# SSD layer: the output projection's first token tile in four steps, y a step sooner, sample state decay inside VectorE's addition

## The chip, the cores and the metric

The kernel runs on one core of a Trainium2 chip. The time is the device time of one launch in microseconds, the median over runs; a run with a profile adds a trace of one execution. The five engines are TensorE (PE in the rows, its weight loads PEld), VectorE (DVE), ScalarE (ACT), GpSimd (POOL) and SyncE (SP), which here issues the DMAs.

## The reference

One inference step of a two-layer decoder: a Mamba-2 SSD layer, then a latent attention (MLA) layer, with a prompt of 1024 tokens and 8 samples of 8 tokens each that go on from a stored state. All is float32. The change lies in the SSD layer (h is 1024 wide, the inner width 2048, 32 heads of 64, 8 groups of 4 heads, state 128, conv of 4 taps):

```python
def ssd_mixer(h, conv_buf, ssm_state, w_in, conv_w, conv_b, dt_bias, a_log, d_skip, norm_w, w_out):
    proj = jnp.einsum('btd,de->bte', h, w_in)                     # z | x B C | dt
    xbc, new_buf = causal_conv(xbc, conv_buf, conv_w, conv_b)     # 4 taps along time
    xbc = jax.nn.silu(xbc)
    ...
    y, new_state = ssd_scan(xs, dt, a_head, bm, cm, ssm_state)    # by chunks of 128 tokens
    # per chunk: s = dec * s + st
    y = (y + d_skip[:, None] * xs) * jax.nn.silu(z)
    y = y * rsqrt(mean(y * y, per group) + eps) * norm_w
    return einsum('bte,ed->btd', y, w_out), new_buf, new_state    # added to h
```

The layer that follows takes h again, normalised, through its own input weights.

## The kernel before, in words

A float32 product is done as three matmuls of rounded halves: each operand x is split into xh (a cast, on ScalarE or by helper line L130) and xl = x - xh (VectorE or GpSimd, helper line L131), and xh*wh, xh*wl and xl*wh are added in a PSUM bank. The order of the instructions on each engine is the order in which the code is written; nothing moves them later. PSUM has eight banks: two tr, two pj, and one each of cb, y, pv and st.

*The groups.* `ssd_groups` runs the groups g = 1 to 7 in 21 steps t each. In a step stand side by side the input projection and conv of group g (`Flow`: matmuls into pj; conv taps on VectorE, L617; Silu on ScalarE, L626 to L631; z, the gate) and the scan of group g-1 (`Scan`). The scan has eight chunks of 128 prompt tokens and a ninth of the 64 sample tokens, two steps for a chunk. At an even step TensorE does `front(i+1)` (transposes into trp, L703 to L706; cb, L708), at an odd one `back(i)` (the chunk's state st, L89; its output py, L759 and L89). Between them ScalarE does the exponentials M (L734, L740) and casts Ch, xddh and Sh, VectorE adds and multiplies (S, y, xD), GpSimd the low halves. The result y of a chunk is stored to DRAM (y_d), and its squares are summed per token (yssq).

In steps 12 to 20 the scan handles the states of the eight samples, four tiles n of 128 x 4 x 128: `turn_state` (PE, into a tr bank named s0p, L856), `split_state` (halves sh and sl; and GpSimd multiplies the state by its decay, L864), `use_state` (products into pv, L877), `next_state` (a product into the st bank, named sn, L882) and `add_state` (VectorE, s = s + sn, L886). sn and the chunks' st share the one st bank. `third(q)` splits, on VectorE (L826, L829), the sample inputs that `next_state` takes.

*The output projection.* After group 7's projection a last loop of 43 steps runs the scan of group 7 (its first 22 steps) with the product y x w_out. This is cut in two over the inner width: oa takes w_out's chunks 0 to 7 (groups 0 to 3; tag a), ob the chunks 8 to 15 (tag b), each over nine token tiles (eight of 128, one of 64). oa starts from x, and ob from what oa has stored in h_d. For a tile i with first step T(i), each step a half hf of 512 columns:

- `load_y` three steps ahead (SP, yt from y_d), `load_x` one ahead;
- `scale` two ahead (ScalarE, four times 128x256, L1016), and in the same step `turn` (eight PE transposes into both tr banks, ytp, L1026);
- `split` one ahead (yh on ScalarE, yl on VectorE);
- `proj`: 24 matmuls of 128x512 into a pj bank (poa or pob, L101), then the eviction that adds the bank to xr (VectorE), and `store` to h_d two steps after the first.

`WOut` brings w_out: a chunk of 128 x 1024 is loaded into a ring of raws (wraw, L1075, 512 KB each), multiplied by the norm weight and cast to woh (ScalarE, L1080), and VectorE makes wol (`low`, L1086). oa's first step is A0 = 5 and ob's B0 = 23: the eight chunks of oa are split in steps 0 to 3, two a step, and the last six of ob in steps 21 and 22.

*What follows.* The MLA layer first turns h (L235, from xt) and multiplies it by its input weights (wraw from in_mla_w_in, L273). The first three tiles of h are loaded during ob's last tiles.

Of the kernel before, what the change touches and what calls it, by code (L numbers as in the profile page):

```python
# [17 lines left out]
D = 1024  # L18
# [506 lines left out]
class Flow:  # L525
# [75 lines left out]
    def ew(self, t):  # L601
# [10 lines left out]
        if t > 11:  # L612
            bi, j = 3, t - 14
# [58 lines left out]
class Scan:  # L672
# [185 lines left out]
    def split_state(self, n):  # L858
        k, q, pr = self.k, *divmod(n, 2)
        self.sh, self.sl = (self.tile([128, 512], "s" + x, f"s{x}{self.g}{n}", 1, F32R) for x in "hl")  # L860
        split(k, self.sh, self.sl, self.s0p)
        h0 = 4 * self.g + 2 * pr
        s0 = self.s0[n]
        k.nc.gpsimd.tensor_tensor(s0, s0, k.decs[:, h0 // 2, 4 * q : 4 * q + 4].unsqueeze(2).to_broadcast([128, 4, 128]),  # L864
                                  op=ALU.mult)
# [19 lines left out]
    def add_state(self, n):  # L885
        self.k.nc.vector.tensor_tensor(self.s0[n], self.s0[n], self.sn.rearrange("p (b n) -> p b n", b=4), op=ALU.add)  # L886

    def ew(self, t, mid=None):
# [14 lines left out]
        if t == 14:  # L903
            self.third(1)
# [25 lines left out]
        if t == 11:  # L930
            self.third(0)
# [62 lines left out]
class OutProj:  # L994
    def __init__(self, k, ypools, ws, psum, k0, load, tag):
        self.k, self.yp, self.ws, self.psum, self.k0, self.load, self.tag = k, ypools, ws, psum, k0, load, tag
# [5 lines left out]
    def load_y(self, i):  # L1002
        k, (t0, m) = self.k, TILES[i]
        y = self.y[i] = self.yp[i].tile([128, self.ng, 256], F32, tag="yt", name=f"yt{self.tag}{i}", bufs=1)
        k.nc.sync.dma_start(y[:m].rearrange("p g c -> p (g c)"),
                            k.y_d[t0 : t0 + m, self.k0 * 128 : (self.k0 + self.nk) * 128])

    def load_x(self, i):
        yp = self.yp[i]
        xr = self.xr[i] = yp.tile([128, D], F32, tag="xr", name=f"xr{self.tag}{i}", bufs=YHB[yp.name])  # L1010
# [18 lines left out]
    def split(self, i):  # L1029
        yp, m = self.yp[i], TILES[i][1]  # L1030
        nb = YHB[yp.name]
        yh, yl = self.yhl[i] = [yp.tile([128, self.nk, 128], F32R, tag="y" + x, name=f"y{x}{self.tag}{i}", bufs=nb)
# [5 lines left out]

    def proj(self, i, hf):
        nc, m = self.k.nc, TILES[i][1]  # L1040
        c = slice(hf * 512, hf * 512 + 512)
        p = self.psum.tile([128, 512], F32, tag="pj", name=f"po{self.tag}{i}{hf}", bufs=PB["pj"])
        (yh, yl), ws, xr = self.yhl[i], self.ws, self.xr[i]
        drain(mm_tok(nc, p, m, 512, [(yh[:, kk, :m], yl[:, kk], yh[:, kk], ws[kk][0][:, c], ws[kk][1][:, c])
                                     for kk in range(self.nk)]))

# [10 lines left out]
    def ew(self, t):  # L1057
        for d, f in ((2, self.store), (-3, self.load_y), (-2, self.scale), (-1, self.load_x), (-1, self.split)):
            i, odd = divmod(t - d, 2)
            if not odd and 0 <= i < 9:  # L1060
                f(i)

    def pe(self, t):
        i, odd = divmod(t + 2, 2)
        if not odd and 0 <= i < 9:
            self.turn(i)


class WOut:
# [3 lines left out]
    def load(self, kk):  # L1073
        raw = self.raw[kk] = load_raw(self.raws, 1, D, self.bufs)[:, 0]
        self.k.nc.sync.dma_start(raw, self.k.I["ssd_w_out"][0][kk * 128 : kk * 128 + 128])  # L1075

    def split(self, kk, pool):
        nc, raw = self.k.nc, self.raw.pop(kk)
        hi, lo = (pool.tile([128, D], F32R, name=f"wo{x}{kk}") for x in "hl")
        nc.scalar.activation(hi, raw, AF.Copy, scale=self.k.ssdn[:, kk : kk + 1])  # L1080
        self.late.append((raw, hi, lo, kk))
        return hi, lo
# [8 lines left out]
def YORD(yb, ya):  # L1091
    return (yb, ya) * 4 + (yb,)


A0, B0 = 5, 23
# [8 lines left out]
def ssd_groups(k, g0, nxt, pools, sp, psum, st, left, right, als):  # L1104
# [6 lines left out]
    for g in range(1, G):  # L1111
        fl, nxt = nxt, Flow(k, g + 1, pools) if g < G - 1 else None
        nscan = Scan(k, fl, (sp, psum))
        for t in range(21):
# [22 lines left out]
            if t == 18 and not nxt:  # L1137
                als.close()
                wrs = ExitStack()
# [12 lines left out]
    ya = st.enter_context(open_pool(tc, name="ya", bufs=1))  # L1152
    wx = st.enter_context(open_pool(tc, name="wox", bufs=1))
    wsa, wsb = [], []
    oa = OutProj(k, (ya,) * 9, wsa, psum, 0, x_loader(k), "a")
    ob = None
    for t in range(B0 + 20):
        ev = None
        for o, T in ((oa, A0), (ob, B0)):
            u = t - T  # L1160
            if o and 0 <= u < 18:
                ev = o.proj(*divmod(u, 2))
        if t < 22:
            scan.ew(t)
        if t == 0:
            pscan.ew(21)
        if t < 4:
            for kk in (2 * t, 2 * t + 1):
                wsa.append(wo.split(kk, wa))
        if t in (5, 6):  # L1170
            wsb.append(wo.split(t + 3, wx))
        if t < 7:
            wo.low()
            for kk in ((3, 4), (5, 6), (7, 8), (9,), (), (), ())[t]:
# [1158 lines left out]
```

## Time and profile before

| | |
|---|---|
| median of three runs | 2117.57 us (2114.17, 2117.57, 2123.74) |
| profiled execution | 2121.48 us, its span 2119.7, mean granted clock of TensorE 0.955 |
| the groups' loop, g = 1 to 7 | about 150 to 843 us |
| the last loop | 843 to 1140, oa until 1020, ob after |
| MLA | 1140 to the end |

A row of a timeline or of the chain has the start in us, the duration in us, the engine and line, what is written from what, and the size; in square brackets stands how long the engine was idle before it and what ended that. A row of the waits has the engine and line that waited, the line waited for, the total in us, how many times, and the longest. A row of a group of instructions has least, median and largest duration in ns, the first and the last start, and the sizes.

### The profile page before, as it was taken

The numbers are of one execution on the slowest core, as the hardware profiler recorded it, in microseconds if no ns is written. First come the engines' busy times: TensorE is split into PE (matmuls) and PEld (weight loads), VectorE is DVE, ScalarE is ACT, GpSimd is POOL, SyncE is SP. The second block draws the span as 40 slices with busy tenths as digits, with TensorE's granted clock in tenths as the row PEclk, the third lists the DMA queues.
The fourth block names the chain that finished last, engine by engine and source line by source line (L and its number), as shares of the span: only waits on it lengthen the run. The fifth ranks groups of instructions, "written<-read, shape, count | busy, mean of one in ns | idle before, by whom it ended". The sixth has DMA issues, their size and how long they took to land.

```text
span 2119.7 us, 33702 instructions
## 1 busy us (share of the span) xinstructions
PE 1947.4 (92%) x12001; PEld 1776.3 (84%) x12001; DVE 1239.8 (58%) x2556; ACT 1110.2 (52%) x2627; POOL 799.8 (38%) x993
## 2 busy tenths in 40 slices
PE   6989999999999999589798999699999999889998
PEld 5879999999999998477687998698888788768887
DVE  4427574757575666534324314366787878776665
ACT  5346666565656666533325324234676667745553
POOL 0327464746464575332000001102333334655551
PEclk9989999999999999699999999899999999989999
DMA  4113322223323333443455332132111212454441
GB/s 143 40 37 89 90 84 83 89 87 87 88 79 90 90 89 103 145 147 126 145 163 168 122 147 66 52 105 69 47 45 40 63 37 78 131 163 139 143 146 44
DMA packets 186479, 206.56 MB, mean 97 GB/s; under 512 B 23132, under 2 KB 151912, under 8 KB 185928
## 3 DMA queue, kind: packets, MB, share of 16 engines
q1 hardware_dynamic: 181480, 185.40, 29.0%
q0 software_dynamic: 4752, 18.88, 2.8%
q8 instruction: 95, 1.56, 0.3%
q14 instruction: 72, 0.59, 0.1%
q10 hardware_dynamic: 80, 0.13, 0.0%
HBM read 151.05 MB, written 53.28 MB: 96 GB/s over the span
## 4 chain that ended last, share of the span: by engine, by line
PE 63%; DVE 12%; ACT 8%; issue 7%; DMA 5%; POOL 4%; SPq 1%; POOLq 0%; DVEq 0%; ACTq 0%
PE pj L89 22%; PE pq L101 5%; PE poa L101 4%; PE pob L101 4%; PE py L759 2%; PE pj L101 2%; POOL kvl L1981 2%; PE pz L101 1%; PE pk L101 1%; ACT acc L626 1%; PE p L101 1%; PE vp L89 1%; DVE tl L1700 1%; PE kp L89 1%; PE st L89 1%
## 5 line engine op out<-in xcount | busy, mean ns | idle before, releaser
L89 PE MATMUL pj<-xh,wih 128*128 128x384 f32 (+1 forms) x768 | 255.7, 337 | 9.4 <-ACT xh L236 4.8
L89 PE MATMUL pj<-xl,wih 128*128 128x384 f32 (+1 forms) x768 | 254.8, 332 | 0.0
L89 PE MATMUL pj<-xh,wil 128*128 128x384 f32 (+1 forms) x768 | 253.1, 330 | 0.0
L131 DVE TENSOR_TENSOR wil<-wraw,wih 128x512 fp32r<-128x512 f32 x88 | 71.0, 809 | 181.4 <-ACT wih L130 181.4
L1700 POOL TENSOR_TENSOR tl<-P,th 128x384 fp32r<-128x384 f32 (+1 forms) x96 | 90.4, 942 | 181.9 <-ACT P L1698 142.6
L89 PEld LDWEIGHTS pj<-xh,wih 128*128 128x128 f32 x768 | 146.2, 191 | 11.0 <-ACT xh L236 5.8
L617 DVE SCALAR_TENSOR_TENSOR acc<-raw,vec,acc 128x1112 f32<-128x1112 f32 x84 | 148.7, 1770 | 0.2
L89 PEld LDWEIGHTS pj<-xl,wih 128*128 128x128 f32 x768 | 146.7, 191 | 0.6
L89 PEld LDWEIGHTS pj<-xh,wil 128*128 128x128 f32 x768 | 146.2, 190 | 0.0
L101 PE MATMUL pj<-wih,xh 128*128 128x256 f32 x504 | 145.6, 293 | 0.0
L101 PE MATMUL pj<-wil,xh 128*128 128x256 f32 (+1 forms) x504 | 141.1, 286 | 0.0
L1697 ACT ACTIVATE th<-st 128x512 fp32r<-128x512 f32 x192 | 94.1, 490 | 72.8 <-PE st L1693 54.7
L101 PE MATMUL pj<-wih,xl 128*128 128x256 f32 x448 | 128.3, 286 | 0.0
L796 POOL TENSOR_TENSOR y<-y,xD 128x256 f32<-128x256 f32 x64 | 83.7, 1308 | 92.2 <-DVE y L795 86.2
L131 POOL TENSOR_TENSOR xddl<-xdd,xddh 128x256 fp32r<-128x256 f32 x64 | 60.7, 948 | 134.6 <-ACT xddh L130 134.6
L1981 POOL TENSOR_TENSOR kvl<-pgr,kvh 128x1024 fp32r<-128x1024 f32 x32 | 77.9, 2434 | 78.8 <-ACT kvh L1980 78.8
L101 PEld LDWEIGHTS pj<-wih,xh 128*128 128x128 f32 x504 | 98.5, 195 | 0.0
L130 ACT CAST Ch<-acc 128x128 fp32r<-128x128 f32 x56 | 16.9, 302 | 153.2 <-PE py L89 153.2
L734 ACT ACTIVATE M<-M,tok 128x128 f32<-128x128 f32 (+1 forms) x288 | 90.5, 388 | 11.3 <-DMA M<-acs_d 11.3
L101 PEld LDWEIGHTS pj<-wil,xh 128*128 128x128 f32 (+1 forms) x504 | 95.2, 189 | 0.6
L1698 ACT ACTIVATE P<-st 128x512 f32<-128x512 f32 x192 | 93.2, 486 | 0.0
L101 PEld LDWEIGHTS pj<-wih,xl 128*128 128x128 f32 x448 | 87.6, 195 | 0.0
(999 smaller groups left out, 6436.4 us busy)
## 6 DMA issues: line engine op xcount, KB each, us to landing
wraw<-in_ssd_w_in SPq DMA_DIRECT2D x92, 256.0 KB
M<-acs_d SPq DMA_DIRECT2D x64, 256.0 KB
y_d<-xD SPq DMA_DIRECT2D x64, 128.0 KB
s<-in_state_ssm SPq DMA_DIRECT2D x32, 256.0 KB
out_s_ssm<-s SPq DMA_DIRECT2D x32, 256.0 KB
wraw<-in_ssd_w_out SPq DMA_DIRECT2D x16, 512.0 KB
q_d<-qt SPq DMA_DIRECT2D x32, 192.0 KB
qp<-q_d SPq DMA_DIRECT2D x8, 768.0 KB
```

Of the source, the lines that this page charges most:

```text
L89: nc.tensor.matmul(out, a, b, start=(i == 0), stop=(i == n - 1))
L101: nc.tensor.matmul(o, a, b, start=(j == 0), stop=(j == len(ops) - 1))
L131: (eng or nc.vector).tensor_tensor(lo, src, hi.bitcast(F32), op=ALU.subtract)
L617: nc.vector.scalar_tensor_tensor(acc, self.raw[bi][:, j : j + n], k.convw[j][:, blk : blk + 1], acc, op0=ALU.mult, op1=ALU.add)
L626: nc.scalar.activation(acc[:, :, :SEQ], acc[:, :, :SEQ], AF.Silu)
L734: nc.scalar.activation(M[:m, h, :m], M[:m, h, :m], AF.Relu, bias=c.tk[:, 0, 4 * g + h : 4 * g + h + 1], scale=-1.0)
L759: nc.tensor.matmul(py[:m, h * 64 : h * 64 + 64], c.M[:m, h, :m], c.xdt[:m, h * 64 : h * 64 + 64], start=True, stop=True)
L796: nc.gpsimd.tensor_tensor(y[:m], y[:m], c.xD[:m], op=ALU.add)
L1697: nc.scalar.activation(th[:, :n], ps[:, :n], AF.Exp, scale=SCALE)
L1698: nc.scalar.activation(P[:, :n], ps[:, :n], AF.Exp, scale=SCALE)
L1700: eng.tensor_tensor(tl[:, :n], P[:, :n], th[:, :n].bitcast(F32), op=ALU.subtract)
L1981: nc.gpsimd.tensor_tensor(rl, raw, rh.bitcast(F32), op=ALU.subtract)
```

## The change

In the groups: the fourth block's three conv taps move from steps 14, 15, 16 to 15, 16, 17; the Silu of the first pair of blocks goes to step 16 from 17, and one of z's two to step 17 from 19; `third(0)` stands at the start of step 11 and not at its end. The decay of the sample states leaves GpSimd: `add_state` does s = s * dec + sn in four VectorE instructions, one for each sample, with the decay as a scalar per partition.

```diff
-            bi, j = 3, t - 14
+            bi, j = 3, t - 15
...
-        if t in (17, 18):
-            acc, xs = self.xc[t - 17]
+        if t in (16, 18):
+            acc, xs = self.xc[t // 2 - 8]
...
-        if t == 19:
-            for z in self.z[:2]:
-                nc.scalar.activation(z, z, AF.Silu)
+        if t in (17, 19):
+            z = self.z[t // 2 - 8]
+            nc.scalar.activation(z, z, AF.Silu)
...
-        k.nc.gpsimd.tensor_tensor(s0, s0, k.decs[:, h0 // 2, 4 * q : 4 * q + 4].unsqueeze(2).to_broadcast([128, 4, 128]),
-                                  op=ALU.mult)
...
     def add_state(self, n):
-        self.k.nc.vector.tensor_tensor(self.s0[n], self.s0[n], self.sn.rearrange("p (b n) -> p b n", b=4), op=ALU.add)
+        q, pr = divmod(n, 2)
+        c, s0 = (4 * self.g + 2 * pr) // 2, self.s0[n]
+        for b in range(4):
+            self.k.nc.vector.scalar_tensor_tensor(s0[:, b], s0[:, b], self.k.decs[:, c, 4 * q + b : 4 * q + b + 1],
+                                                  self.sn[:, 128 * b : 128 * b + 128], op0=ALU.mult, op1=ALU.add)
...
-        if t == 14:
-            self.third(1)
+        if t in (11, 14):
+            self.third(t == 14)
```

On VectorE, in the scan of group 1 from step 14 to 15, before (y and xD are the chunk's output, acc the conv's sum, s the sample state, sl its low half):

```order
L794 TENSOR_TENSOR y_6_3464<-py_6_3397,tok 128x256
L795 TENSOR_TENSOR y_6_3464<-y_6_3464,py_6_3397 128x256
L617 SCALAR_TENSOR_TENSOR acc_3033<-raw_3043,vec,acc_3033 128x1112
L886 TENSOR_TENSOR s_3153<-s_3153,sn_3480 128x512
L131 TENSOR_TENSOR sl_3510<-s0p_3475,sh_3509 128x512
L721 TENSOR_TENSOR xdt_8_3518<-trp_8_3470,tok 64x256
L727 TENSOR_TENSOR cbm_8_3520<-cb_8_3473,masks 64x64
L803 TENSOR_TENSOR xD_6_3390<-y_6_3464,z_2324 128x256
L617 SCALAR_TENSOR_TENSOR acc_3033<-raw_3043,vec,acc_3033 128x1112
```

and after:

```order
L794 TENSOR_TENSOR y_6_3471<-py_6_3404,tok 128x256
L795 TENSOR_TENSOR y_6_3471<-y_6_3471,py_6_3404 128x256
L885 SCALAR_TENSOR_TENSOR s_3161<-s_3161,decs,sn_3486 128x128 x4
L131 TENSOR_TENSOR sl_3519<-s0p_3481,sh_3518 128x512
L721 TENSOR_TENSOR xdt_8_3526<-trp_8_3476,tok 64x256
L727 TENSOR_TENSOR cbm_8_3528<-cb_8_3479,masks 64x64
L803 TENSOR_TENSOR xD_6_3397<-y_6_3471,z_2328 128x256
L617 SCALAR_TENSOR_TENSOR acc_3041<-raw_3051,vec,acc_3041 128x1112
```

The first tap of acc now stands behind the state's addition and the split of the next state.

In the output projection: each tile's `scale` comes a step ahead of its `turn`, and `load_y` five ahead. A tile 0 takes four steps in place of two: `part(q)` does both halves of two chunks, 12 matmuls, and holds both pj banks; tile i from 1 on starts at T + 2 + 2i. A0 is 1 and B0 is 21. The first tile of a is loaded at step 18 of group 7, scaled at 20, turned right after the last projection of group 7 and split in step 0.

```diff
+        self.start = [T] + [T + 2 + 2 * i for i in range(1, 9)]
...
+    def part(self, q):
+        nc, ws = self.k.nc, self.ws
+        yh, yl = self.yhl[0]
+        if q == 0:
+            self.po = [self.bank(0, hf) for hf in range(2)]
+        for hf, p in enumerate(self.po):
+            c = slice(hf * 512, hf * 512 + 512)
+            for kk in (2 * q, 2 * q + 1):
+                wh, wl = (x[:, c] for x in ws[kk])
+                for j, (a, b) in enumerate(((yh, wh), (yh, wl), (yl, wh))):
+                    nc.tensor.matmul(p, a[:, kk], b, start=(kk + j == 0), stop=(kk == 7 and j == 2))
+        if q == 3:
+            return [self.evict(0, hf, p) for hf, p in enumerate(self.po)]
+        return []
...
-        for d, f in ((2, self.store), (-3, self.load_y), (-2, self.scale), (-1, self.load_x), (-1, self.split)):
+        for d, f in ((-1, self.split), (-3, self.scale), (-1, self.load_x), (-5, self.load_y)):
...
-A0, B0 = 5, 23
+A0, B0 = 1, 21
```

w_out has four raws ahead and not three: chunks 0 to 3 are loaded at step 18 of group 7, 4 to 7 in steps 0 and 1; 8 and 9 at step 8, split at 10 and 11; 10 and 11 loaded there, split at 21; 12 to 15 all loaded at 21 into four raws, split at 22 and 23, into the tiles of a's chunks. y has one ring of two for a and b.

```diff
-                wo = WOut(k, wrs.enter_context(open_pool(tc, name="wor", bufs=1, side="right")), 3)
-                for kk in range(3):
-                    wo.load(kk)
+                wo = WOut(k, wrs.enter_context(open_pool(tc, name="wor", bufs=1, side="right")), 4)
+                wo.load(0, 1, 2, 3)
+            if t == 20 and not nxt:
+                oa.scale(0)
...
+    oa.turn(0)
...
+            w2, wo = wo, WOut(k, st.enter_context(open_pool(tc, name="wor3", bufs=1, side="right")), 4)
+            wo.load(12, 13, 14, 15)
+            ob.ws += w2.split(wa, 10, 11)
+            w2.low()
+        if t in (22, 23):
+            ob.ws += wo.split(wa, 2 * t - 32, 2 * t - 31)
+            wo.low()
...
-        if ev:
-            ev()
+        if t >= B0:
+            evs += ob.work(t)
         if t < 21:
             scan.pe(t)
+        if A0 <= t < A0 + 4:
+            evs += oa.work(t)
+        for ev in evs:
+            ev()
```

On TensorE, at the end of group 7's steps and the start of the last loop, before (sn ends group 6's scan, trp, cb, st and py are the scan of group 7, pj and poa are projections):

```order
L101 MATMUL pj_20_10499<-wil,xh 64x256
L101 MATMUL pj_20_10499<-wih,xh 128x256
L882 MATMUL sn_10546<-bb6True,x36True 128x512
L703 MATMUL trp_1_10585<-ident,acc_9766 128x128
L704 MATMUL trp_1_10585<-ident,acc_9766 128x128
L706 MATMUL trp_1_10585<-ident,acc_9359 128x128
L708 MATMUL cb_1_10589<-acc_9359 128x128
L89 MATMUL st_0_10626<-xddh_0_10564,BTh_0_10528 128x256
L89 MATMUL st_0_10626<-xddl_0_10565,BTh_0_10528 128x256
L89 MATMUL st_0_10626<-xddh_0_10564,BTl_0_10529 128x256
L759 MATMUL py_0_10627<-xdt_0_10531,M_0_10372 128x64 x4
```

and after:

```order
L878 MATMUL sn_10607<-bb6True,x36True 128x512
L1025 MATMUL ytpa_10609<-ident,yta_10485 128x128 x4
L1025 MATMUL ytpa_10614<-ident,yta_10485 128x128 x4
L703 MATMUL trp_1_10666<-ident,acc_9814 128x128
L704 MATMUL trp_1_10666<-ident,acc_9814 128x128
L706 MATMUL trp_1_10666<-ident,acc_9407 128x128
L708 MATMUL cb_1_10670<-acc_9407 128x128
L89 MATMUL st_0_10707<-xddh_0_10632,BTh_0_10585 128x256
L89 MATMUL st_0_10707<-xddl_0_10633,BTh_0_10585 128x256
L89 MATMUL st_0_10707<-xddh_0_10632,BTl_0_10586 128x256
L759 MATMUL py_0_10708<-xdt_0_10588,M_0_10424 128x64 x4
L1050 MATMUL poa_10716<-woh_10652,yha_10644 128x512
```

Tile 0's eight transposes now stand ahead of the scan's second front, and its first products (12 in all, of which the first is shown) right behind the first chunk's py.

On ScalarE, in the scan's fifth chunk before (yta is a tile of y to be scaled, yha its high half):

```order
L130 CAST Ch_5_11104<-acc_9359 128x128
L734 ACTIVATE M_5_11029<-M_5_11029,tok 128x128 x4
L804 ACTIVATE y_3_11042,yssq<-xD_3_10963 128x256
L1016 ACTIVATE yta_11048<-yta_11048,yssq 128x256 x4
L740 ACTIVATE M_5_11029<-M_5_11029 128x512
L130 CAST xddh_5_11180<-xdd_5_11100 128x256
L130 CAST Sh_4_11185<-S_5_11090 128x256
L130 CAST yha_11199<-ytpa_11139 128x512
L130 CAST yha_11199<-ytpa_11144 128x512
```

and after, in the third chunk, where tile 1 of a is split:

```order
L130 CAST Ch_3_10938<-acc_9407 128x128
L734 ACTIVATE M_3_10846<-M_3_10846,tok 128x128 x4
L804 ACTIVATE y_1_10859,yssq<-xD_1_10799 128x256
L740 ACTIVATE M_3_10846<-M_3_10846 128x512
L130 CAST xddh_3_11004<-xdd_3_10934 128x256
L130 CAST Sh_2_11009<-S_3_10924 128x256
L130 CAST yha_11019<-ytpa_10965 128x512
L130 CAST yha_11019<-ytpa_10970 128x512
L1015 ACTIVATE yta_10877<-yta_10877,yssq 128x256 x4
L716 COPY xsT_4_11067<-trp_4_11033 128x256
L719 CAST BTh_4_11069<-trp_4_11033 128x128
```

The four scales stood behind the M of the chunk and ahead of the split of the same tile; now they are those of the next tile and come behind the split.

At the MLA start SP issued the first in_mla_w_in loads right behind the store of ob's tile 7 and ahead of tile 8's; after the change they stand behind both.

More of the change, by code (lines that the diff above doesn't have):

```diff
@@ L1071, in __init__, with load, split @@
         self.k, self.raws, self.bufs, self.raw, self.late = k, raws, bufs, {}, []
[L1073 to L1082, printed above, removed]
+    def load(self, *kks):
+        for kk in kks:
+            raw = self.raw[kk] = load_raw(self.raws, 1, D, self.bufs)[:, 0]
+            self.k.nc.sync.dma_start(raw, self.k.I["ssd_w_out"][0][kk * 128 : kk * 128 + 128])
+    def split(self, pool, *kks):
+        nc = self.k.nc
+        out = []
+        for kk in kks:
+            raw = self.raw.pop(kk)
+            hi, lo = (pool.tile([128, D], F32R, tag=f"wo{x}{kk % 8}", name=f"wo{x}{kk}", bufs=1) for x in "hl")
+            nc.scalar.activation(hi, raw, AF.Copy, scale=self.k.ssdn[:, kk : kk + 1])
+            self.late.append((raw, hi, lo, kk))
+            out.append((hi, lo))
+        return out
     def low(self):
```

129 lines of the change are left out of this document (60 added, 69 removed).

## The prediction

> **What bounds the kernel now.** I read the page first, then four stretches of the span in the windows view, then who TensorE waits for in each of them, and last the chain of waits and the timelines at the places that the change touches.
>
> ```profile
> span 2119.7 us, 33702 instructions
> PE 1947.4 (92%) x12001; PEld 1776.3 (84%) x12001; DVE 1239.8 (58%) x2556; ACT 1110.2 (52%) x2627; POOL 799.8 (38%) x993
> ```
>
> TensorE is busy 92% of the span, so only its idle time and its slow-clock time can be won. The stretches below are the eight groups' loop from 150 us, the start and middle of the output projection's loop, its second half, and the start of the MLA layer (columns: us, PE, PEld, DVE, ACT, POOL, granted clock, DMA share, GB/s).
>
> ```profile
> 150.00:843.00 693.00, 672.92 (x4929) 661.54 (x4927) 451.78 (x780) 426.44 (x1131) 403.20 (x574) 0.99 0.30 87
> 843.00:1045.00 202.00, 155.87 (x771) 126.73 (x770) 89.25 (x162) 84.71 (x206) 55.26 (x78) 0.86 0.44 140
> 1045.00:1140.00 95.00, 95.00 (x447) 77.33 (x446) 22.74 (x37) 22.80 (x49) 0.90 (x2) 1.00 0.48 153
> 1140.00:1180.00 40.00, 32.65 (x179) 28.79 (x178) 24.30 (x43) 25.69 (x49) 3.19 (x3) 0.91 0.64 209
> ```
>
> The groups leave 20.1 us idle, the projection's first 202 us leave 46.1 idle and 28 more to a clock of 0.86 (0.14 x 202), its second half leaves nothing, and the MLA start leaves 7.4. That is the room: about 100 us, of which this change aims at most.
>
> **The groups (taps a step later, no POOL decay, third(0) earlier).** What TensorE waits for between 150 and 843:
>
> ```profile
> PE st L89 <- DVE s L886: 12.7, 7, 1.8
> PE s0p L856 <- DVE b L829: 4.4, 7, 0.7
> PE pv L877 <- DVE sl L131: 2.7, 6, 0.5
> ```
>
> Those 19.8 us are nearly the whole 20.1, seven times each, once per group. One group in the timelines of VectorE, GpSimd and TensorE, with two windows after it:
>
> ```profile
> 309.53 3.99 DVE L617 SCALAR_TENSOR_TENSOR acc<-raw,vec,acc 128x1112 f32<-128x1112 f32 x1
> 313.44 0.67 DVE L886 TENSOR_TENSOR s<-s,sn 128x512 f32<-128x512 f32 x1
> 315.44 1.36 DVE L617 SCALAR_TENSOR_TENSOR acc<-raw,vec,acc 128x1112 f32<-128x1112 f32 x1
> 311.31 1.03 POOL L864 TENSOR_TENSOR s<-s,decs 128x512 f32<-128x512 f32 x1
> 314.26 0.35 PE L89 MATMUL st<-xddh,BTh 128*128 128x256 f32 x1 [1.81 <-DVE s L886]
> 314.00:318.00 4.00, 3.74 (x27) 3.77 (x28) 3.97 (x10) 1.08 (x4) 0.57 (x1) 0.71 0.34 98
> 318.00:322.00 4.00, 4.00 (x31) 3.85 (x31) 1.82 (x3) 0.88 (x2) 2.18 (x2) 0.86 0.22 66
> ```
>
> The conv tap of step 14 stands in VectorE's queue ahead of the addition to the sample state, takes 3.99 us there against 1.36 for the tap two steps on, and the one st bank comes free only after it: TensorE stands 1.81 us. Then the clock is below full for two windows (0.29 x 4 + 0.14 x 4 = 1.7 us lost). With the tap behind the addition the state is added up to 3.99 us sooner, more than the 1.81 that TensorE waits, so this wait goes: 12.7. What is late next is the tap itself: the last one moves to step 17, but the Silu that needs it is that of acc1 in step 18, and the other Silu is moved ahead to share out ScalarE's work. The pv wait shrinks, since sl stands behind the same tap: I take 1 of 2.7. The s0p wait is for a bank that the last product of third(0) frees, which now comes ahead of front1 on VectorE; what front1 issues is then late by the same 0.4 to 0.7 us, so I take 2 of 4.4. The clock is 0.99 over 693 us, 7 us lost in all; seven windows like the two above would be 12, so I take the 7. Sum 22.7, and I say 22.
>
> The new addition costs VectorE four instructions of 128x128 with a scalar operand in place of one of 0.67 us. Before has none of this size; the nearest of this operation is
>
> ```profile
> L237 DVE SCALAR_TENSOR_TENSOR xl<-xtp,vec,xh x24: 550/617/619, 17.5 to 56.6; 128x384 fp32r<-128x384 f32 x16, 128x320 fp32r<-128x320 f32 x8
> ```
>
> 67 ns per 64 columns: about 0.35 us at 128 columns, 1.4 for four, so 0.7 more than now, 32 times. Below, four cost at least what one does (0.67); above, four times 0.55. It lies in a stretch where VectorE works 452 of 693 us, and is less than the tap that leaves its place, so I put it at nothing on the path. The GpSimd multiply (1.03 each) leaves an engine that is idle 40% here: nothing by itself, but fewer stretched taps. Ends for the groups: 27 (all waits and clock), and 10 (the taps, up to 3.99 us long, hold up TensorE at another place for half of what they do now).
>
> **The start of the last loop.** What TensorE waits for between 843 and 1045, three of its rows, then pieces of the chain of waits, then one window in the columns above:
>
> ```profile
> PE ytpa L1026 <- ACT yta L1016: 19.5, 6, 7.9
> PE ytpb L1026 <- ACT ytb L1016: 10.2, 1, 10.2
> PE trp L703 <- DVE yla L131: 2.7, 1, 2.7
> ```
>
> ```profile
> 851.43 1.05 ACT woh L1080
> 855.01 4.25 DMA wraw<-in_ssd_w_out
> 861.74 2.18 ACT woh L1080 x2
> 865.91 6.25 DMA yta<-y_d
> 872.18 1.71 ACT yta L1016 x4
> 878.77 7.20 PE poa L101 x24
> 892.83 7.00 PE poa L101 x24
> 900.38 5.49 PE poa L101 x24
> ```
>
> ```profile
> 860.00:870.00 10.00, 3.32 (x14) 3.06 (x14) 6.80 (x11) 6.97 (x14) 4.64 (x6) 0.50 0.75 220
> ```
>
> Here TensorE has little to do and runs at 0.50, since no product of the projection may begin before all eight halves of w_out are split and tile 0 is loaded, scaled and turned; then it does tile 0's 48 products in two pieces at that clock or near it (7.20 and 7.00 against 5.49). After the change these 48 lie in the four steps of the split, 12 behind each two chunks. The loads of w_out (four raws ahead, not three) take away the 4.25, and tile 0 loaded in group 7 the 6.25. What is left is ScalarE's queue, in order, from where woh began: tile 0's scale and the casts of its split come ahead of it (1.7 and about 1, so 851.4 becomes 854.2), eight woh of 1.09 (8.7), tile 1's scale (1.7), and the scan's own work (6.97 busy in that window less four woh leaves 2.6 for two steps; with its waits for VectorE I put 7 for four): 871.6. Then the fourth step's exponentials, casts and state, from the end of the scale to the first product 4.9 us before (873.9 to 878.8): 876.5. Twelve products at half clock take about 5 (24 took 7.20 and 5.49, part warm and warm, so 2.7 to 3.6 at those clocks and 5.5 at twice the warm time): 881.5. The decay matrices' loads on SP now stand behind four chunks at once; I add 3 for them, near the 4.25 that a chunk cost here, so tile 1 begins near 885 and not 900.4: 15, and I take **14** for a turn more on the way. Ends: 25 (all waiting gone, clock full) and 5 (the chunks' transfers bind, so only the twelve last products are moved).
>
> **Tiles 1 to 7.** The scale of a tile now comes one step ahead of its turn. Before, both were in one step:
>
> ```profile
> 925.41 0.30 ACT L130 CAST Ch<-acc 128x128 fp32r<-128x128 f32 x1 [6.61 <-PE py L89]
> 927.20 1.69 ACT L1016 ACTIVATE yta<-yta,yssq 128x256 f32<-128x256 f32 x4
> ```
>
> ScalarE is idle for 6.61 us, then has the scan's casts and exponentials to do, and only behind them the four scales that the turn waits for. One step earlier they fall in such an idle time, or behind the M product, and TensorE turns at once. Of the 19.5 us, 7.9 are tile 0's; 9.7 of the rest lie behind 900, and the clock of that stretch loses about 3. I take **10**. Ends: 16 (all of both) and 3 (front's own bank is late next: the trp wait for yla, 2.7 at its longest, each second tile).
>
> **From a to b.** The first turn of b waited 10.2 us, and the last chunks of w_out came late as raws came free one at a time:
>
> ```profile
> 1029.15 1.97 PE L1026 MATMUL ytpb<-ident,ytb 128*128 128x128 f32 x8 [10.16 <-ACT ytb L1016]
> 1037.27 1.15 ACT L1080 ACTIVATE woh<-wraw,vec 128x1024 fp32r<-128x1024 f32 x1 [3.45 <-DMA wraw<-in_ssd_w_out]
> 1039.51 1.15 ACT L1080 ACTIVATE woh<-wraw,vec 128x1024 fp32r<-128x1024 f32 x1 [1.09 <-DMA wraw<-in_ssd_w_out]
> 1009.38 5.68 PE poa L101 x24
> 1043.64 11.04 PE pob L101 x48
> ```
>
> Tile 8 of a began about 1015.1 (1009.38 + 5.68) and b's tile 1 at 1049.2 (1043.64 + half of 11.04): 34 us. After, b's tile 0 is loaded, scaled and turned under a's last tiles, and its products follow the split chunk by chunk. But chunks 12 to 15 can be loaded only at step 21, when the scan's room comes free. Of the last two the second was split 2.2 us behind the first, and a chunk's transfer took 4.25 at the start. With two stores ahead of them I put the four at 6.3, 8.5, 10.7 and 12.9 after the step's start, woh and wol of the last 1.15 + 1.29, the last eight products 2.7: 18 after the step's start, which itself stands 10 behind tile 8's start. That is 28: a gain of **6**. Ends: 10 (the ytpb wait in full) and 0 (the four transfers share the way with y, xr and h stores).
>
> **The MLA start.** The work is the same, but tile 8 of b is stored by SP from a ring of two, and the first MLA weights stand in SP's queue behind the last store and not behind tile 7's:
>
> ```profile
> 1133.55 8.46 SPq L273 DMA_DIRECT2D wraw<-in_mla_w_in  x5
> 1142.36 0.47 SPq L1055 DMA_DIRECT2D h_d<-xrb  x1
> 1138.31 1.05 ACT L130 CAST wgh<-wraw 128x1024 fp32r<-128x1024 f32 x1 [11.21 <-DMA wraw<-in_mla_w_in]
> 1145.21 5.73 DMA xt<-h_d
> ```
>
> The last store waits for the last product's eviction (about 1140), so the first weights are issued some 6 us later, are first cast 4.8 after that (1138.31 - 1133.55), and TensorE has only 24 turns of h to do meanwhile. Against it the three later tiles of h are asked for ahead of the weights, and their 5.73 goes. I take **0**; ends -6 and +4.
>
> **The sum.** 22 + 14 + 10 + 6 + 0 = 52 us. The profiled execution took 2121.5 us (span 2119.7 and 1.8 around it), which is 3.9 above the median of the three runs; nothing ties that to a stage, so I take the 52 off the median: 2117.6 - 52 = 2066. The ends added up are 12 and 82.
>
> **The rule that speaks against the clock term.** The rows say that the clock fell to 0.71 in the window after a 1.81 us gap. The Trainium skill, "TensorE: Matmul & The Clock Gate", Part 1: The HAM clock gate, has it that the array drops to half rate only after an idle window of about 3.4 us. By that rule a gap of 1.81 would not slow it, and the 7 us of clock in the groups would have another cause and stay. The trace disagrees here, as the fall stands right behind the gap, so I keep the 7 and hold the other as a rival.
>
> **Rivals.**
> - *The group wait only moves.* The tap takes up to 3.99 us wherever GpSimd works beside it; at step 15 it may stand ahead of another product that TensorE waits for, or four additions may stretch as the tap does (times 2.9: 4 us). For it: the stretch of this very tap. Against: the later tap was 1.36, and one GpSimd operation beside it is gone. Of 22 about 20 are lost: 2086.
> - *Transfers bind.* Chunks and decay matrices share SP and the DMA engines, which are at 0.75 and 220 GB/s from 860 to 870 already. The start gives 4 and not 14, the transition 0, the MLA start -4: 52 - 10 - 6 - 4 = 32: 2086.
> - *The clock of the groups stays* for another cause: 52 - 7 = 45: 2073.
> - *Slower: every tile's split holds up the scan.* The turn fills both tr banks, and the scan's next front waits until ScalarE and VectorE have emptied them. Before, the longest such wait was 2.7 us. To undo 52 it must be 7.4 us in each of seven tiles, and 9 to be slower by 0.5%: 52 - 63 = -11, 2129. Against it: ScalarE, which begins the split, idles 6.61 us of a pair, so I hold it unlikely.
>
> **Chances.** My forecast 0.60, its own range 2050 to 2082; the group wait only moves 0.14; transfers bind 0.13; the clock stays 0.07; slower 0.04; about 0.02 for two of the small ones together. The range takes in the first four: 2046 (half of the terms near their upper ends) to 2090. A difference of 0.5%, 10.6 us, is about what a measurement of this kernel tells from no change; all cases but the last two lie beyond it: faster 0.93, within 0.03, slower 0.04.
>
> **What would show it.** In the profile after: no wait of st for the state's addition in the groups and their stretch shorter by some 20 us (if it is there with other names: the first rival); 12 poa products behind each pair of woh from about 855, the clock there above 0.50, and poa's 5.5 us blocks from a time 36 us earlier than before (22 + 14); hardly a wait of ytpa for yta; b's first products waiting for wol and not for ytb; the first MLA weight issued behind the last h store. I am wrong if VectorE's four additions are late for the st bank, if the taps are still 4 us and something else waits behind them, or if trp waits for yla at every tile.

## The result, and the profile after

The changed kernel takes 2052.48 us (median of four runs, 2045.65 to 2054.24), the kernel before 2118.06: 65.6 us less, a ratio of 0.9682 with the 95% interval 0.9651 to 0.9714. Forecast were 2066 in a range of 2046 to 2090. The profiled execution has a span of 2052.5 us. Its page, first rows:

```profile
span 2052.5 us, 33717 instructions
PE 1932.4 (94%) x12001; PEld 1765.2 (86%) x12001; DVE 1228.3 (60%) x2652; ACT 1111.3 (54%) x2627; POOL 768.2 (37%) x961
```

The windows of the same stretches (columns as before the change: us, PE, PEld, DVE, ACT, POOL, granted clock, DMA share, GB/s), the groups, oa, ob and the MLA start:

```profile
150.00:813.50 663.50, 662.71 (x4919) 652.65 (x4918) 441.66 (x860) 427.28 (x1129) 373.06 (x543) 1.00 0.31 90
813.50:967.40 153.90, 135.96 (x721) 113.80 (x720) 75.58 (x156) 73.10 (x190) 48.69 (x70) 0.93 0.48 166
966.00:1078.00 112.00, 108.05 (x503) 86.08 (x501) 39.70 (x64) 35.72 (x71) 3.55 (x7) 1.00 0.45 163
1078.00:1118.00 40.00, 36.02 (x209) 31.56 (x208) 23.19 (x41) 24.07 (x46) 2.83 (x4) 0.96 0.66 201
```

The groups leave 0.8 us idle where they left 20.1, and the clock stands at 1.00. In the groups no wait of TensorE is left that the view lists. Behind them it lists these for the output projection:

```profile
PE trp L703 <- DVE yla L131: 15.5, 4, 6.8
PE pob L1050 <- DVE wol L1124: 2.6, 4, 0.8
PE ytpa L1025 <- ACT xddh L130: 1.6, 1, 1.6
PE pob L1050 <- ACT woh L1117: 1.4, 1, 1.4
PE ytpa L1025 <- ACT yta L1015: 0.7, 1, 0.7
```

The waits for the scale (ytpa 19.5, ytpb 10.2) are gone but for 0.7, as said; the wait of the scan's front (trp) for a tile's split has grown from 2.7 to 15.5, which was the mechanism of the rival on the slower side: 12.3 of it in two places at the start, 3.2 among the tiles behind.

To see where the 67 us between the two spans lie I use the same instruction in both traces. The second of group 6's four sn marks the end of the groups, the first poa or pob block of tile 1 the two projections, s0p in the changed kernel the end of a's tile 7, kpt a place in the MLA start, and pt a place late in that layer. First the rows of before:

```profile
830.25 0.48 PE L882 MATMUL sn<-bb6False,x36False 96*128 96x512 f32 x1
L1802 PE MATMUL kpt<-ident,kprows x32: 270/272/273, 1183.9 to 1228.8; 128*128 128x128 f32 x32
L2008 PE MATMUL pt<-ident,P x128: 270/273/473, 1828.0 to 2087.5; 128*128 128x128 f32 x128
```

then those of the changed kernel (timeline, chain of waits, lines by tile):

```profile
801.04 0.48 PE L878 MATMUL sn<-bb6False,x36False 96*128 96x512 f32 x1
853.00 5.45 PE poa L101 x24
960.61 0.44 PE s0p L856 x4
988.11 5.48 PE pob L101 x24
1064.90 13.04 PE pob L101 x56
L1830 PE MATMUL kpt<-ident,kprows x32: 270/272/273, 1117.5 to 1162.4; 128*128 128x128 f32 x32
L2036 PE MATMUL pt<-ident,P x128: 270/273/474, 1767.3 to 2020.2; 128*128 128x128 f32 x128
```

| stage | forecast gain | measured | from the marks |
|---|---|---|---|
| groups | 22 (10 to 27) | 29.2 | 830.25 - 801.04 |
| start of the last loop, to tile 1 | 14 (5 to 25) | 18.2 | 900.4 - 853.0 = 47.4, less 29.2 |
| tiles 1 to 7 of a | 10 (3 to 16) | 7.1 | 1015.1 - 960.6 = 54.5 |
| from a to b's tile 1 | 6 (0 to 10) | 6.6 | 1049.2 - 988.1 = 61.1 |
| b's tiles and the MLA start | 0 (-6 to 4) | 5.3 | 1183.9 - 1117.5 = 66.4 |
| rest of the MLA layer | none | 0.8 | 2119.7 - 2052.5 = 67.2 |

In the table, 900.4 is the third row of poa in the chain that the prediction shows, and 1015.1 and 1049.2 are worked out there. The last row is small as a whole only: from kpt to pt's first the changed kernel took 649.8 us against 644.1, from pt's first to the end 285.2 against 291.7, in code that is the same. Over the traces of all the kernels here the first of these stretches took from 635.2 to 649.8, so below I go by marks, and by the medians only for 10 us and more. The groups repeat far better: in seven traces with the changed kernel's groups, six groups took 585.65 to 585.90 us.

### The profile page after: what moved, and what is told of

The parts are those of the page before. It is cut to its first block, busy times and chain, and to the rows that moved or that the text cites. A ratio compares the mean times of both kernels' runs of the same rounds, so it can differ in the third digit from the quotient of the medians.

```text
span 2052.5 us, 33717 instructions
## 1 busy us (share of the span) xinstructions
PE 1932.4 (94%) x12001; PEld 1765.2 (86%) x12001; DVE 1228.3 (60%) x2652; ACT 1111.3 (54%) x2627; POOL 768.2 (37%) x961
## 4 chain that ended last, share of the span: by engine, by line
PE 71%; DVE 10%; DMA 5%; issue 5%; POOL 4%; ACT 4%; SPq 1%; POOLq 0%; DVEq 0%; ACTq 0%
PE pj L89 21%; PE pj L101 8%; PE pq L101 5%; PE pob L101 4%; PE poa L101 4%; PE py L759 3%; POOL kvl L2009 2%; PE pz L101 1%; PE pk L101 1%; PE p L101 1%; PE sc L1682 1%; PE vp L89 1%; PE st L89 1%; PE st L1714 1%; PE st L1716 1%
## 5 line engine op out<-in xcount | busy, mean ns | idle before, releaser
L617 DVE SCALAR_TENSOR_TENSOR acc<-raw,vec,acc 128x1112 f32<-128x1112 f32 x84 | 130.3, 1551 | 0.2
L130 ACT CAST Ch<-acc 128x128 fp32r<-128x128 f32 x56 | 16.9, 302 | 155.8 <-PE py L89 155.8
```

The costliest lines, as they stand in the source:

```text
L617: nc.vector.scalar_tensor_tensor(acc, self.raw[bi][:, j : j + n], k.convw[j][:, blk : blk + 1], acc, op0=ALU.mult, op1=ALU.add)
```

## The experiments

### The groups: each edit undone

**g1, taps back in steps 14 to 16.**

```diff
-            bi, j = 3, t - 15
+            bi, j = 3, t - 14
```

> The changed kernel with one edit undone: the three conv taps of the fourth block are in steps 14, 15, 16 again; all else as changed (four short additions, no decay on GpSimd, third(0) first). Queue theory: the tap ahead of the state's addition is what holds the st bank, whatever its length, so the wait of st for s comes back seven times, 0.5 to 1.8 us each, and with it the clock: 2052 + 10 to 23 = 2062 to 2075. Stretch theory: what made the tap long was GpSimd's decay multiply beside it; that is gone, the tap takes 1.4 us and the addition is still in time: no wait, 2050 to 2056.

2048.03 us (ratio to before 0.967, 0.9633 to 0.9707): nothing lost by the medians; by the marks (the first sn of group 0 to the first of group 6) six groups took 588.2 us against 585.7. **g2, the decay back on GpSimd** and one addition:

```diff
+        k.nc.gpsimd.tensor_tensor(s0, s0, k.decs[...].to_broadcast([128, 4, 128]), op=ALU.mult)
...
-        for b in range(4):
-            self.k.nc.vector.scalar_tensor_tensor(s0[:, b], s0[:, b], self.k.decs[...], self.sn[...], op0=ALU.mult, op1=ALU.add)
+        self.k.nc.vector.tensor_tensor(self.s0[n], self.s0[n], self.sn.rearrange(...), op=ALU.add)
```

> The changed kernel with the decay back on GpSimd (one multiply of 128x512) and one addition of 128x512 on VectorE; the taps stay in steps 15, 16, 17. Queue theory: the addition is free of the tap, so at most it waits for the multiply, which ended 0.1 us before TensorE needed the bank in the group shown: some 0.6 us a group, 2052 to 2060. Stretch theory: the multiply beside VectorE's work stretches it again and the wait of st comes back at 1 us or more a group with its clock: 2060 to 2075.

2050.38 us (0.9687, 0.9651 to 0.9724): nothing lost either, and by the marks six groups took 584.4 us, 1.3 less than with the four additions. So of the two theories neither holds alone: the tap ahead of the addition costs little while it is short, and the multiply costs nothing while the tap stands behind the addition. **g3, third(0) at the end of step 11:**

```diff
-        if t in (11, 14):
-            self.third(t == 14)
+        if t == 14:
+            self.third(1)
...
+        if t == 11:
+            self.third(0)
```

> The changed kernel with third(0) at the end of step 11 again. If its place made the s0p wait (0.63 us a group, 4.4 in all), that wait comes back by name and the time is 2054 to 2060; if that wait went only because VectorE's queue is shorter now, nothing comes back: 2050 to 2054.

2049.66 us (0.9676, 0.964 to 0.9713). The s0p wait is back by name, 4.4 us in seven groups, but six groups took only 1.7 us more (587.4 against 585.7). No single edit of the three is needed for most of what the groups gained, and with the taps moved the decay's move gains nothing. **g4, these edits alone** in the kernel before (the first diff of the change: taps, Silu, addition, third; nothing of the projection):

> The kernel before with the groups' edits alone (taps, Silu places, four short additions, no GpSimd decay, third(0) first); the output projection as before. The traces give the groups 29 us (a mark at their end went from 838.57 to 809.36): 2118 - 29 = 2089, 2084 to 2095, if that gain stands by itself. If the projection's edits (tile 0 turned at the groups' end, the earlier loads) are part of it or the last loop takes some of it back: 2095 to 2110.

2083.93 us (0.9853, 0.9809 to 0.9897), 33.7 less than before. The mark of the groups stands at 803.1, 27.1 us earlier than in before. The groups' gain stands by itself.

### The groups: one edit alone, and two undone

**g5, taps and decay both undone** in the changed kernel (the diffs of g1 and g2 together).

> The changed kernel with both undone: taps in steps 14, 15, 16 and the decay on GpSimd, one addition; third(0) stays first. Lost-turns theory: the tap was 4 us long because it lost its turn to GpSimd operations that followed each other without a gap, the decay multiply among them, and only the tap ahead of the addition made that a wait; either edit cures it, both undone bring it back: tap near 4.0 at its longest, st wait 1 us or more in each of seven groups, 2052 + 15 to 25 = 2067 to 2077. Rival: it is third(0)'s place that shifts VectorE against GpSimd so that they no longer meet: no long tap, 2048 to 2056.

2062.41 us (0.974, 0.97 to 0.9781), 10 more than the changed kernel, a little under the forecast. The wait of st is there again to the last digit; then VectorE's and GpSimd's timelines of a group:

```profile
PE st L89 <- DVE s L886: 12.7, 7, 1.8
```

```profile
307.79 3.99 DVE L617 SCALAR_TENSOR_TENSOR acc<-raw,vec,acc 128x1112 f32<-128x1112 f32 x1
311.70 0.67 DVE L886 TENSOR_TENSOR s<-s,sn 128x512 f32<-128x512 f32 x1
...
308.18 0.73 POOL L131 TENSOR_TENSOR Sl<-S,Sh 128x256 fp32r<-128x256 f32 x1
308.87 0.73 POOL L796 TENSOR_TENSOR y<-y,xD 128x256 f32<-128x256 f32 x1
309.57 1.03 POOL L864 TENSOR_TENSOR s<-s,decs 128x512 f32<-128x512 f32 x1
310.57 1.69 POOL L776 TENSOR_TENSOR S<-S,decp 128x256 f32<-128x256 f32 x1
```

The same place in g1, where the tap stands ahead of the addition too but the multiply is gone, and g1's wait of st:

```profile
306.95 1.73 DVE L617 SCALAR_TENSOR_TENSOR acc<-raw,vec,acc 128x1112 f32<-128x1112 f32 x1
307.47 1.82 POOL L796 TENSOR_TENSOR y<-y,xD 128x256 f32<-128x256 f32 x1
```

```profile
PE st L89 <- DVE s L885: 1.3, 7, 0.2
```

In g5 GpSimd is at an operation when the tap begins, and does the rest of it, then Sl, y and the multiply without a gap; only then does L776 take 1.69 us in place of 0.62, its median before, and the tap ends. These lengths fit two engines of which one at a time has its turn: the tap lost it for four operations, then held GpSimd up in turn. In g1 GpSimd had idled for 0.39 us ahead of Sl (its row at 306.77); there it is GpSimd's y that is held (1.82), and the tap is through after 1.73 us. But operations that follow each other without a gap are not enough for a long tap. In g6, described next, the multiply is still there, GpSimd works without a gap before and beside the tap in its later place, and the tap takes 1.73 us as in g1:

```profile
310.15 1.73 DVE L617 SCALAR_TENSOR_TENSOR acc<-raw,vec,acc 128x1112 f32<-128x1112 f32 x1
309.91 0.80 POOL L776 TENSOR_TENSOR S<-S,decp 128x256 f32<-128x256 f32 x1
310.67 1.68 POOL L748 TENSOR_TENSOR xD<-xsT,dsk 128x256 f32<-128x256 f32 x1
```

So what decides which engine gets the turn stays open. What is shown is where the long tap occurs: once in each of the seven groups of before and of g5, which have the old place and the multiply both; in g1, g2, g6, g7 and the changed kernel, which lack one or both, no tap of L617 is longer than 1.79 us. Either edit cures it.

**g6, the taps alone,** and **g7, the decay inside the addition alone,** each in the kernel before (g6 is `t - 14` to `t - 15`, g7 the change's lines of `split_state` and `add_state`):

> The kernel before with the fourth block's taps in steps 15, 16, 17 alone (decay on GpSimd, third(0) last, Silu places as before). Lost-turns theory: the st wait goes and with it the slow clock; s0p's 4.4 stays: 2118 - 20 to 28 = 2090 to 2098. Rival: the decay must go as well: under 10 gained, 2108 to 2118.

> The kernel before with the decay in VectorE's addition alone (taps in 14, 15, 16, third(0) last). Lost-turns theory: the tap keeps its place but is about 1.7 us long and the st wait falls under 0.3 a group: 2118 - 18 to 28 = 2090 to 2100. Rival: the four short additions behind the tap hold the bank as long as the tap did: 2108 to 2118.

2096.61 us (0.9902, 0.9869 to 0.9934), 20.5 less; and 2090.5 us (0.9865, 0.9831 to 0.9899), 26.6 less. Each alone brings most of g4's 33.7, and the two are not to be added. In g6 the wait of st is gone and those of s0p and pv stay; in g7 st is at 0.2 a group. The windows of six groups, from the first sn of group 0 to the first of group 6, for before, the changed kernel, g5, g6 and g7:

```profile
208.51:818.14 609.63, 592.09 (x4330) 582.15 (x4328) 395.31 (x688) 376.24 (x997) 351.05 (x502) 0.99 0.30 86
```

```profile
206.75:792.47 585.72, 585.05 (x4327) 576.34 (x4326) 386.97 (x760) 378.14 (x997) 326.16 (x478) 1.00 0.31 90
```

```profile
207.95:806.18 598.23, 586.67 (x4330) 578.06 (x4328) 394.22 (x688) 377.36 (x997) 355.09 (x502) 1.00 0.30 88
```

```profile
208.19:799.44 591.25, 584.63 (x4329) 575.64 (x4328) 390.21 (x688) 376.53 (x997) 352.42 (x502) 1.00 0.31 89
```

```profile
206.31:797.38 591.07, 586.13 (x4328) 575.80 (x4327) 388.63 (x760) 375.48 (x997) 325.23 (x478) 1.00 0.31 89
```

Length less PE's busy time is idle time: 17.5 us before, 0.7 after, 11.6 in g5, 6.6 in g6 and 4.9 in g7. PE's own busy time for the same work shows what the clock adds: 592.1 before against 585.1 after, 7.0 us, but only 1.6 in g5, which has the same st waits. The granted clock says the same. In the 24 us from 2 us ahead of the first sn of each of the seven groups it was, before, 1.00, 0.93, 0.93, 1.00, 0.86, 1.00 and 0.93, which is 1.7 us lost where it is 0.93 and 3.4 where it is 0.86; in g5 it was 0.93 in groups 2 and 6 and 1.00 in the others; in g1, g3, g6, g7 and the changed kernel it was 1.00 in all seven. So the clock fell in no group of a kernel without the gap of 1.8 us, and with it in four of seven groups before and in two of seven in g5. In these runs the gap is needed for the fall, and it is not enough.

What g5 keeps of the groups' edits, third(0) first and the Silu places, is not nothing beside this gap: its six groups are 11.4 us shorter than before's, 6.0 by idle time (s0p and pv wait no more) and 5.4 by PE's busy time.

### The output projection

**p3, a's tile 0 summed in the fourth step alone:**

```diff
-        if T <= t < T + 4:
+        if T <= t < T + 4 and self.tag == "a":
+            return [e for q in range(4) for e in self.part(q)] if t == T + 3 else []
+        if T <= t < T + 4:
             return self.part(t - T)
```

> The changed kernel with the 48 products of a's tile 0 all in the fourth step of the split; loads, turn and split of tile 0 as changed. If summing under the split is what the start won, 36 products move behind it at 0.23 us each: 2052 + 8 = 2060 (2056 to 2068, with a colder clock). If the start won by the earlier loads and the earlier y alone, and TensorE waits out the same ScalarE work in any case: 2050 to 2055.

2062.98 us (0.9749, 0.972 to 0.9778), 10.5 more than the changed kernel; its chain of waits at the place:

```profile
834.44 6.06 DMA M<-acs_d
850.52 13.18 PE poa L1050 x48
863.70 5.45 PE poa L101 x24
```

From the groups' mark (802.9) to tile 1 it is 60.8 us, against 52.0 in the changed kernel: 8.8 us of the start's 18.2 are the products under the split. The other 9.4 are the earlier y and what else stands earlier; no run parts them. One cause is small: **p4, three raws again,**

```diff
-                wo = WOut(k, wrs.enter_context(open_pool(tc, name="wor", bufs=1, side="right")), 4)
-                wo.load(0, 1, 2, 3)
+                wo = WOut(k, wrs.enter_context(open_pool(tc, name="wor", bufs=1, side="right")), 3)
+                wo.load(0, 1, 2)
...
-            if t < 2:
-                wo.load(2 * t + 4, 2 * t + 5)
+            if t < 3:
+                wo.load(*((3, 4), (5, 6), (7,))[t])
```

> The changed kernel with three raws for w_out's chunks 0 to 7 as before (0 to 2 ahead, 3 and 4 at step 0, 5 and 6 at step 1, 7 at step 2). If the fourth raw took away the wait for a chunk (4.25 us in the kernel before), 3 to 6 us come back: 2055 to 2058. If ScalarE's queue is what the start waits for: 2048 to 2054.

2052.08 us (0.9698, 0.9651 to 0.9745): nothing lost by the medians, and tile 1 begins 52.8 us behind the groups' mark, against 52.0. The wait for a chunk is in p4's chain again, but where it stands the changed kernel has one of like length for y; first p4's row, then the changed kernel's:

```profile
831.56 5.27 DMA wraw<-in_ssd_w_out
828.99 5.00 DMA yta<-y_d
```

The fourth raw takes one wait for a transfer away, and another takes its place.

**p1, the scale in the step of the turn:**

```diff
-        for d, f in ((-1, self.split), (-3, self.scale), (-1, self.load_x), (-5, self.load_y)):
+        for d, f in ((-1, self.split), (-2, self.scale), (-1, self.load_x), (-5, self.load_y)):
```

> The changed kernel with each tile's scale in the step of its turn again, two steps ahead of its first product (tile 0 of a, placed by hand, stays). If the earlier scale is what took the waits of ytpa away, 1.5 us or so come back at each of a's tiles 1 to 7 and about 3 at b's first: 2052 + 7 to 14 = 2059 to 2066. If those waits went because ScalarE is freer without the POOL and tap stalls: 2048 to 2055.

2064.82 us (0.974, 0.9689 to 0.9791), 12.3 more. Its waits from tile 1 of a to b:

```profile
PE ytpa L1025 <- ACT yta L1015: 11.5, 5, 3.3
PE ytpa L1025 <- ACT xddh L130: 1.4, 1, 1.4
```

The earlier scale is worth as much as I gave all of this stage, and more. What the stage lost elsewhere shows in the changed kernel's windows of tile 2, of tile 4 and of the first half of tile 5:

```profile
867.00:881.00 14.00, 14.00 (x76) 12.00 (x75) 6.05 (x14) 6.22 (x19) 5.61 (x9) 1.00 0.51 179
896.00:913.50 17.50, 15.11 (x84) 12.81 (x84) 9.16 (x20) 7.96 (x23) 6.85 (x12) 1.00 0.55 194
913.50:926.00 12.50, 10.91 (x60) 9.21 (x59) 4.13 (x10) 3.88 (x13) 3.24 (x6) 0.86 0.53 190
```

Tile 2 takes 14.0 us with TensorE full, but in the second and third row TensorE idles 2.4 and 1.6 us, and in the third the clock is at 0.86. By the chain of waits, w_out's chunks 8 and 9 are split just ahead of these places, in between the scan's work (woh at 891.9 and 905.3); in the kernel before these two were split ahead of tile 1. No run takes them away, so this cause is read and not shown.

**p2, the split of a's tiles ahead of the scan's work:**

```diff
-                if t == T + d and not (i == 0 and self.tag == "a" and d < 0):
+                if t == T + d and not (self.tag == "a" and (d == -1 and f == self.split or i == 0 and d < 0)):
...
+        for i, T in enumerate(oa.start):
+            if t == T - 1:
+                oa.split(i)
         if t < 22:
             scan.ew(t)
...
-            oa.split(0)
```

> The changed kernel with the split of a's tiles (casts on ScalarE, low halves on VectorE) ahead of the scan's work of the same step and not behind it. The trace after shows TensorE waiting 15.5 us in four places for yla, since both tr banks are full until the split is done and the scan's front needs one. If that wait ends with the split, 8 to 13 us go: 2039 to 2045. If the scan's exponentials, now a split later, are what TensorE needs next, the wait only changes its name: 2048 to 2056.

2046.47 us (0.9655, 0.961 to 0.97), 6.0 less than the changed kernel. The trp wait falls from 15.5 to 6.1, other waits of 1 to 2 us come in, and b's end comes 4.2 us earlier than in the changed kernel: half of the least that I expected, the rest changed its name. Its chain of waits at the place:

```profile
832.97 6.19 DMA M<-acs_d
846.41 4.56 PE poa L1050 x12
850.97 5.47 PE poa L101 x24
```

**b1, p2 with chunks 6 and 7 loaded behind the scan's M of step 2:**

```diff
-            if t < 2:
-                wo.load(2 * t + 4, 2 * t + 5)
+            if t in (0, 2):
+                wo.load(t + 4, t + 5)
```

> The kernel with the split of a's tiles ahead of the scan's work (as in p2), and w_out's chunks 6 and 7 loaded at step 2, behind that step's decay matrix M on SP, and not at step 1 ahead of it. In p2 the chain has 6.19 us for that M load, where a chunk of 512 KB for two stood ahead of it. If the place in SP's queue makes that price, 3 to 5 us go: 2041 to 2044 (p2 had 2046). If the chunks, now later, become what ScalarE waits for instead: 2045 to 2050.

2045.13 us (0.9648, 0.9618 to 0.9678). In its chain the M load is gone and tile 1 begins earlier:

```profile
826.08 4.19 DMA wraw<-in_ssd_w_out
843.96 2.75 PE poa L1050 x12
846.71 5.70 PE poa L101 x24
```

From the groups' mark (800.0) to tile 1 it takes 46.7 us, against 49.6 in p2 and 52.0 in the changed kernel: the M load's place on SP was worth 2.9 by these two traces, near what I had put on it. Both kernels lie below the changed one by their marks; by the times their intervals overlap with its own.

## Why the prediction was right, and where its steps were off

- *Which waits go.* Right: st, s0p and pv in the groups, ytpa and ytpb behind them, all by name. The sign and the order of the terms came out as worked.
- *The sum, 52, measured 67.2 by the traces* and 65.6 by the medians: 7.2 more in the groups, 4.2 at the start, 2.9 less in tiles 1 to 7, 0.6 more from a to b, 5.3 at the MLA start and 0.8 in the rest. Two of the five terms lie beyond their own upper ends. That the time is in the range all the same is owed to its lower end, which stood for half of the terms near their upper ends.
- *The groups, 22, measured 29.2, over my upper end of 27.* The 29.2 are 16.9 of idle time and 7.0 of PE's busy time in six groups, 3.5 from the first sn of group 6 to the mark, and 1.8 by which the first sn of all already stood earlier. These 1.8 are not the change's: that place lies between 205.8 and 208.9 in all the traces. Without them it is 27.4, still a little over. I took 2 of s0p's 4.4 and 1 of pv's 2.7, for fear that front1 would be late instead; both went whole by name (4.1 more), though third(0)'s place alone was worth no more than 1.7 in six groups (g3). The clock gave in six groups what I had taken for seven.
- *The clock's rival* (the loss has another cause and stays) fell with g6: there the wait of st alone is gone, and the clock is 1.00 in all seven groups. But I took the fall to follow every gap, as in group 1; it followed four of seven.
- *The reason for the groups' gain* was half of the cause. I called the tap's place the cause and the GpSimd multiply "nothing by itself"; g7 gains 26.6 from the multiply's removal with the tap in its old place, and g1 shows that the place alone costs 0.4 us a group. With the taps moved, the multiply is worth nothing indeed (g2). The rival that the wait only moves failed because no tap is long in its new place: 1.36 us in the changed kernel's group 1, and 1.73 in g6.
- *The four additions:* 1.11 us together by the trace of the group, where I had 1.4; hidden, as said, but for 1.3 us in six groups (g2).
- *The start, 14, measured 18.2.* In the range. The price of 3 for the scan's loads behind the chunks was right (b1: 2.9, beside p2); but the 4.25 of a chunk and the 6.25 of y, which I counted as taken away, left a transfer of 5.00 in the chain, and p4 shows that the fourth raw is worth 0.8 and not 4.25.
- *Tiles 1 to 7, 10, measured 7.1.* The scale's move was right and worth more (p1), but the step left out chunks 8 and 9, which the change puts among these tiles, and made too little of the trp wait, which is 3.2 there. That the chunks cost this is read from the chain, not shown.
- *From a to b, 6, measured 6.6,* and b's first tile waits for wol, as said.
- *The MLA start, 0, with b's tiles 5.3, over my upper end of 4.* The delay came, somewhat longer than worked: the first weight was cast 6.9 us behind the last product, where it had been 1.5 ahead of it before. But it was paid for once, and the start as a whole was shorter: from the start of the last pob product to kpt it took 41.7 to 44.9 us in the traces with before's beginning (before, g4, g6, g7), and 39.7 to 41.2 with the new one (all others). I had priced the delay and not what stood behind it: 7.4 us of idle and 3.6 of clock in before's window of 40 us, 4.0 and 1.6 after. Which of the waits behind it gave this, no run shows.

## What to carry to other kernels

A wait that repeats once per group at a fixed length is worth a look at the other engine's queue too: here an instruction was long only beside one row of a second engine's operations, and either taking one operation out of that row or taking the instruction out of the way was enough, so that two good edits gave hardly more than one. Undo them singly and together before you credit either. When a bank is held by several engines' steps (turn, cast, low half), put those steps first in their queues: what frees the bank should not stand behind work that nobody waits for yet.

## What the runs showed of the hardware

- VectorE's tap (two inputs in SBUF) of 1.36 us took 3.99 beside GpSimd operations that followed each other, in seven groups of before and of g5, while the addition with its second input in PSUM stayed at 0.67 to 0.69 in before, all 32 times. The Trainium skill, "SBUF — State Buffer", section Who interferes with whom, has it that a VectorE instruction with two SBUF inputs and a GpSimd one that reads SBUF exclude each other, and that at most one SBUF input avoids it; the trace agrees. That the loser waited out not one but four instructions in a row is what I had not expected; in g1 and g6 it got its turn after one.
- The same gap of 1.8 us lowers the clock in some groups and not in others. Before, the windows behind the gap in groups 2 and 3:

```profile
416.00:420.00 4.00, 3.62 (x27) 3.65 (x28) 3.96 (x10) 1.08 (x4) 0.68 (x2) 0.76 0.12 37
518.00:522.00 4.00, 3.60 (x34) 3.63 (x35) 3.96 (x10) 1.09 (x4) 0.71 (x2) 1.00 0.33 98
```

  The rule of the Trainium skill that I weighed in the prediction ("TensorE: Matmul & The Clock Gate", Part 1: The HAM clock gate: an idle window of about 3.4 us) is not met by this gap of 1.8, and yet the clock fell in group 2; in group 3 and in five of g5's seven groups it did not. What decides between them stays open.
